# Batch norm over 64 tiles: moving columns between VectorE's first piece and ScalarE's piece

## The chip, the cores and the metric

The kernel runs on 1 core of one Trainium2 chip. The metric is the time of one launch in device microseconds (us), lower is better; a profiled execution also gives a span, from its first to its last instruction. The engines that do work here are VectorE (DVE in the profile), ScalarE (ACT), SyncE (SP, which only waits and issues transfers) and the core's 16 DMA engines, which move data between device memory and the on-chip buffers.

## The reference

```python
def setup_inputs():
    n = 32
    c = 256
    h = 128
    w = 128
    return {
        "x": np.random.randn(n, c, h, w).astype(np.float32),
...
def reference(
...
    eps = 1e-5
    mean = running_mean.reshape(1, -1, 1, 1)
    var = running_var.reshape(1, -1, 1, 1)
    gamma = gamma.reshape(1, -1, 1, 1)
    beta = beta.reshape(1, -1, 1, 1)
    return gamma * (x - mean) / np.sqrt(var + eps) + beta
```

With the statistics given, this is one multiply and one add for each element, with a scale and a shift for each channel. 537 MB are read and 537 MB written.

## The kernel before

The array is seen as 64 tiles (32 images by 2 blocks of 128 channels). A tile has 128 partitions, one channel each, and 16384 columns of float32, so a row is 64 KB and a tile 8.39 MB. Three buffers `bufs[0..2]` hold three tiles; tile i lives in buffer i mod 3 and is worked on in place. Ahead of the loop the kernel loads the parameters, turns them and computes `scale_t` and `shift_t` (lines 109 to 126); the first three tiles are loaded without a wait for a buffer (lines 90 to 99).

Four queues run after that, each in an order written out by hand, tied together by semaphores:

- VectorE (lines 155 to 158) works on a tile in two pieces. The first, columns 0 to `VFIRST`, waits until the tile has landed and raises `vfirst`. The second, columns `VFIRST` to `VMOST`, raises `vdone`. Tile 0 has one piece (`VHEAD` columns), and the last tile's second piece ends at `VLAST`.
- SyncE (lines 161 to 164) issues the load of tile i when the store of tile i - 3 is complete (line 163) and `vfirst` has been raised for tile i - 1 (line 164). So a load is issued only after the load ahead of it has landed and VectorE's first piece of it is done.
- ScalarE (lines 166 to 173) waits until the store of tile i - 1 is complete (line 168, all but the first and the last two tiles), does the columns from `VMOST` to the end, waits for `vdone` of tile i (line 170), and issues the store of tile i from its own queue (line 171).
- The loads run on the DMA queue that the profile calls q1, the stores on q10; both are spread over the same 16 DMA engines.

So at any time there is at most one load and one store under way. The length of VectorE's first piece lies between a load's landing and the next load's issue, and the length of ScalarE's piece lies between a store's completion and the next store's issue.

Of the kernel before, what the change touches and what calls it, by code (L numbers as in the profile page):

```python
# [8 lines left out]
NBUF = 3  # L9
PAD = 936  # L10
NHEAD = 3
VFIRST = 2560
VMOST = 14336
VHEAD = 8192
VLAST = 9216

# [2 lines left out]
def kernel(  # L19
# [54 lines left out]
    with tc.tile_critical():  # L74
# [26 lines left out]
        def landed(i):  # L101
            if i < NHEAD:
                return first[i], 16
            s = i % NBUF
            before = 1 if s < NHEAD else 0
            return loaded[s], 16 * (i // NBUF + 1 - before)
# [23 lines left out]
        def vector_part(i, first_col, end):  # L130
            t, cb = bufs[i % NBUF], i % NCB
            return nc.vector.tensor_scalar(  # L132
                out=t[:, first_col:end],
                in0=t[:, first_col:end],
                scalar1=scale_t[:, cb : cb + 1],
                scalar2=shift_t[:, cb : cb + 1],
                op0=mybir.AluOpType.mult,
                op1=mybir.AluOpType.add,
            )

        def scalar_part(i, first_col):
            t, cb = bufs[i % NBUF], i % NCB
            return nc.scalar.activation(  # L143
                out=t[:, first_col:],
                in_=t[:, first_col:],
                func=mybir.ActivationFunctionType.Identity,
                bias=shift_t[:, cb : cb + 1],
                scale=scale_t[:, cb : cb + 1],
            ).then_inc(adone, 1)

        def gone(i):
            return stored[i % NBUF], 16 * (i // NBUF + 1)
# [3 lines left out]
        for i in range(1, NT):  # L156
            vector_part(i, 0, VFIRST)._wait_ge(*landed(i)).then_inc(vfirst, 1)
            vector_part(i, VFIRST, VLAST if i == last else VMOST).then_inc(vdone, 1)

# [6 lines left out]
        for i in range(NT):  # L166
            if 0 < i < NT - 2:
                nc.scalar.wait_ge(*gone(i - 1))
            scalar_part(i, VHEAD if i == 0 else VLAST if i == last else VMOST)._wait_ge(*landed(i))
            nc.scalar.wait_ge(vdone, i + 1)  # L170
# [37 lines left out]
```

## Time and profile before

| what | value |
|---|---|
| time, median of 3 runs | 2486.29 us (2485.91 to 2487.04) |
| time of the profiled execution | 2487.21 us |
| its span | 2485.4 us |
| read and written | 536.94 MB and 536.87 MB, 432 GB/s over the span |
| median time from issue to landing | load 37.0 us, store 36.5 us |
| VectorE's pieces, columns and mean time | 2560: 1.61 us; 11776: 6.41 us |
| ScalarE's piece, columns and mean time | 2048: 2.09 us |

The profile's page lists busy time by engine, the DMA queues with the share of the 16 engines' time that their packets took, the chain of work that ended last, and groups of equal instructions by line with the idle time before them and what ended it (`<-DMA out_dram<-t` is a wait for a store, `<-DMA t<-in_x_dram` one for a load). In the rows in order of time, `ACTq` and `SPq` mark the issue of a transfer by ScalarE and SyncE, and x4 a row in which four are merged.

### The profile page before, as it was taken

The page shows a single profiled execution, that of the slowest core. Times are in us where ns is not written, and L with a number is a line of the kernel's source. Part 1 is how long each engine was busy: PE and PEld are TensorE (multiplying, and loading weights), DVE is VectorE, ACT ScalarE, POOL GpSimd, SP SyncE. Part 2 cuts the span into 40 slices and gives each one's busy share as a digit, 9 for nine tenths or more (in the row PEclk, how much of TensorE's full clock was granted, in tenths as well). Part 3 has the DMA queues.
Part 4 walks back from the last instruction along what each step waited for, and adds up shares of the span by engine and source line. Part 5 has one row for each costly group of instructions (what it writes and reads, how often), then busy time and mean ns, then how long its engine had stood idle before and what let it go on. Part 6 is the DMA issues. An engine that isn't in the chain of part 4 may idle for free.

```text
span 2485.4 us, 578 instructions
## 1 busy us (share of the span) xinstructions
DVE 505.3 (20%) x138; ACT 144.9 (6%) x66; POOL 0.2 (0%) x4
## 2 busy tenths in 40 slices
DVE  2122121221212212122121121211212212122120
ACT  1000000000000000000000000000000000000001
POOL 0000000000000000000000000000000000000000
DMA  9999999999999999999999999999999999999999
GB/s 421 424 439 438 422 439 433 428 438 436 426 438 437 425 438 437 428 436 436 437 427 437 436 427 438 431 429 439 423 438 437 433 429 436 437 428 437 435 428 405
DMA packets 18708, 1073.85 MB, mean 432 GB/s; under 512 B 2128, under 2 KB 2192, under 8 KB 2192
## 3 DMA queue, kind: packets, MB, share of 16 engines
q1 hardware_dynamic: 9488, 536.94, 50.0%
q10 hardware_dynamic: 9216, 536.88, 49.9%
q14 instruction: 4, 0.03, 0.0%
HBM read 536.94 MB, written 536.87 MB: 432 GB/s over the span
## 4 chain that ended last, share of the span: by engine, by line
DMA 93%; DVE 4%; another core or an unknown queue 1%; ACT 0%; issue 0%; SPq 0%; DVEq 0%
DMA t<-in_x_dram 93%; DVE t L132 4%; ACT t L143 0%; SPq L93 0%; DVE rows L91 0%; SPq L97 0%; DVE eps_t L109 0%; DVEq L203 0%; SPq L74 0%
## 5 line engine op out<-in xcount | busy, mean ns | idle before, releaser
L132 DVE TENSOR_SCALAR t<-t,scale_t,shift_t 128x11776 f32<-128x11776 f32 (+2 forms) x127 | 501.8, 3993 | 1938.8 <-DMA t<-in_x_dram 1938.7
L143 ACT ACTIVATE t<-t,shift_t,scale_t 128x2048 f32<-128x2048 f32 (+1 forms) x64 | 143.3, 2239 | 2299.2 <-DMA out_dram<-t 2243.3
L110 DVE STREAM_TRANSPOSE turned<-rows 32x1024 f32<-32x1024 f32 x1 | 1.2, 1232 | 12.0 <-DMA rows<-in_running_mean_dram 12.0
L116 ACT ACT_TABLE_LOAD x1 | 1.3, 1283 | 0.9 <-SPq L74 0.9
L91 DVE MEMSET rows<- 32x1024 f32 x1 | 0.9, 912 | 1.2 <-SPq L74 1.2
L116 ACT ACTIVATE std_t<-par,eps_t 128x2 f32<-128x2 f32 x1 | 0.3, 295 | 14.1 <-DVE par L114 14.1
L114 DVE COPY par<-turned 32x8 f32<-32x8 f32 x4 | 0.6, 162 | 0.1
L123 DVE RECIPROCAL rstd_t<-std_t 128x2 f32<-128x2 f32 x1 | 0.2, 165 | 0.4 <-ACT std_t L116 0.4
L125 DVE TENSOR_TENSOR ms_t<-par,scale_t 128x2 f32<-128x2 f32 x1 | 0.2, 161 | 0.0
L126 DVE TENSOR_TENSOR shift_t<-par,ms_t 128x2 f32<-128x2 f32 x1 | 0.2, 161 | 0.0
L124 DVE TENSOR_TENSOR scale_t<-par,rstd_t 128x2 f32<-128x2 f32 x1 | 0.2, 160 | 0.0
L192 POOL MEMSET const-bfloat16-1.0<- 128x1 bf16 x1 | 0.1, 101 | 0.0
L192 POOL MEMSET const-uint8-127<- 128x1 uint8 x1 | 0.1, 101 | 0.0
L192 POOL MEMSET const-float32-0.0<- 128x1 f32 x1 | 0.1, 98 | 0.2 <-issue 0.2
L192 POOL MEMSET const-float32-1.0<- 128x1 f32 x1 | 0.1, 98 | 0.0
L109 DVE MEMSET eps_t<- 128x1 f32 x1 | 0.1, 59 | 0.1
## 6 DMA issues: line engine op xcount, KB each, us to landing
t<-in_x_dram SPq DMA_DIRECT2D x2, 4096.0 KB, 15.9
out_dram<-t ACTq DMA_DIRECT2D x64, 36.5
t<-in_x_dram SPq DMA_DIRECT2D x63, 37.0
rows<-in_running_var_dram SPq DMA_DIRECT2D x1, 16.0 KB, 11.2
rows<-in_gamma_dram SPq DMA_DIRECT2D x1, 16.0 KB, 11.1
rows<-in_beta_dram SPq DMA_DIRECT2D x1, 16.0 KB, 10.8
rows<-in_running_mean_dram SPq DMA_DIRECT2D x1, 16.0 KB, 10.7
```

The lines of the kernel that those rows point to most:

```text
L91: zeroed = step(nc.vector.memset(rows[:], 0.0))
L109: step(nc.vector.memset(eps_t[:], eps))
L110: step(nc.vector.transpose(out=turned[:], in_=rows[:]), fetched, 16 * NPAR)
L114: placed = step(nc.vector.tensor_copy(out=flat[q * B : (q + 1) * B], in_=blocks[:, :, q, 0]))
L116: nc.scalar.activation(out=std_t[:], in_=var_t, func=mybir.ActivationFunctionType.Sqrt, bias=eps_t[:], scale=1.0,)._wait_ge(vec, placed).t ...
L123: step(nc.vector.reciprocal(out=rstd_t[:], in_=std_t[:]), act, 1)
L124: step(nc.vector.tensor_mul(out=scale_t[:], in0=gamma_t, in1=rstd_t[:]))
L125: step(nc.vector.tensor_mul(out=ms_t[:], in0=mean_t, in1=scale_t[:]))
L126: ready = step(nc.vector.tensor_sub(out=shift_t[:], in0=beta_t, in1=ms_t[:]))
L132: return nc.vector.tensor_scalar(out=t[:, first_col:end], in0=t[:, first_col:end], scalar1=scale_t[:, cb : cb + 1], scalar2=shift_t[:, cb ...
L143: return nc.scalar.activation(out=t[:, first_col:], in_=t[:, first_col:], func=mybir.ActivationFunctionType.Identity, bias=shift_t[:, cb : ...
L192: nc = _bacc.Bacc("TRN2", target_bir_lowering=False, num_devices=1)
```

## The change

Two constants. VectorE's first piece has 1696 columns in place of 2560 and its second 11136 in place of 11776; ScalarE's piece has 16384 - 12832 = 3552 columns in place of 2048. The first tile's pieces are as before; in the last tile the border between VectorE's two pieces moves with `VFIRST`.

```diff
--- before.py
+++ after.py
@@ -9,8 +9,8 @@
 NBUF = 3
 PAD = 936
 NHEAD = 3
-VFIRST = 2560
-VMOST = 14336
+VFIRST = 1696
+VMOST = 12832
 VHEAD = 8192
 VLAST = 9216
 
```

## The prediction

> **What bounds the kernel now.** I read the page's queue table first, then the chain of waits, then the groups of instructions, and last one stretch in order of time.
>
> ```profile
> span 2485.4 us, 578 instructions
> DVE 505.3 (20%) x138; ACT 144.9 (6%) x66; POOL 0.2 (0%) x4
> q1 hardware_dynamic: 9488, 536.94, 50.0%
> q10 hardware_dynamic: 9216, 536.88, 49.9%
> DMA t<-in_x_dram 93%; DVE t L132 4%; ACT t L143 0%; SPq L93 0%; DVE rows L91 0%; SPq L97 0%; DVE eps_t L109 0%; DVEq L203 0%; SPq L74 0%
> ```
>
> Loads (q1) take 50.0% and stores (q10) 49.9% of the time of the 16 DMA engines. Together that is 99.9%: they never stand still. The chain is loads, with VectorE's first piece (4%) between them. Taken alone it would say that a shorter first piece saves time; with the engines at 99.9% there is no time to save, only time to lose.
>
> ```profile
> L132 DVE TENSOR_SCALAR t<-t,scale_t,shift_t 128x11776 f32<-128x11776 f32 x62 | 397.2, 6407 | 0.0
> L143 ACT ACTIVATE t<-t,shift_t,scale_t 128x2048 f32<-128x2048 f32 x62 | 129.8, 2093 | 2250.8 <-DMA out_dram<-t 2243.3 <-DMA t<-in_x_dram 7.5
> L132 DVE TENSOR_SCALAR t<-t,scale_t,shift_t 128x2560 f32<-128x2560 f32 x63 | 101.6, 1612 | 1938.7 <-DMA t<-in_x_dram 1938.7
> L143 ACT ACTIVATE t<-t,shift_t,scale_t 128x8192 f32<-128x8192 f32 x1 | 7.2, 7212 | 6.8 <-DMA t<-in_x_dram 6.8
> L132 DVE TENSOR_SCALAR t<-t,scale_t,shift_t 128x8192 f32<-128x8192 f32 x1 | 4.5, 4546 | 0.1
> ```
>
> These are the groups with shapes kept apart (busy, mean ns of one, idle before). They price the change. In order of time:
>
> ```profile
> 1004.96 2.09 ACT L143 ACTIVATE t<-t,shift_t,scale_t 128x2048 f32<-128x2048 f32 x1 [36.56 <-DMA out_dram<-t]
> 1007.08 0.34 ACTq L171 DMA_DIRECT2D out_dram<-t  x1
> 1014.58 7.93 DVE L132 TENSOR_SCALAR t<-t,scale_t,shift_t 128x2560 f32<-128x2560 f32 x2 [30.69 <-DMA t<-in_x_dram]
> 1016.22 116.35 SPq L164 DMA_DIRECT2D t<-in_x_dram  x4
> 1043.71 2.09 ACT L143 ACTIVATE t<-t,shift_t,scale_t 128x2048 f32<-128x2048 f32 x1 [36.66 <-DMA out_dram<-t]
> ```
>
> Two loops run side by side. Store ends, ScalarE works 2.09 us, next store is issued (1007.08). Load ends, VectorE works 1.61 us, next load is issued (1016.22, the first of four merged into that row). Both have a period of 38.64 us (tiles 13 to 14, say). A tile is 128 rows of 64 KB each way, 8 load packets and 8 store packets for each of 16 engines, so a **slot** is 38.64/16 = 2.415 us; the trace's own packet records give 2.418 for nearly all of them. I chained those records, end to start, into 16 engines. In the steady state nearly every engine repeats this (L a load packet, S a store packet):
>
> ```
> LLLL SSSS LSLSLSLS LLLL SSSS LSLSLSLS ...
> ```
>
> So a store's turnaround is hidden by four load packets, and a load's by four store packets: 4 x 2.415 = 9.66 us each. Measured from the last packet's end on the last engine:
> - Store: 2.83 us to ScalarE's start, 2.09 of work, 0.04 to the issue: 4.96. Data then flows 2.85 to 3.3 after the issue. I take that from first store packets that began earlier than about 3.0 after their issue: they were stretched by up to 1.1 us, and ended as if begun at 2.8 to 3.3, a few of some 130 at 3.6 to 3.73; those that began later took the plain 2.418. Sum 7.8 to 8.3 of 9.66: 1.4 to 1.8 spare.
> - Load: 2.79 to VectorE's start, 1.61, 0.03: 4.43. It takes its turn in the alternation about 3.56 after the issue (3.4 to 3.75: the side on which engines give it a fifth store packet first, or not). Sum 7.99. To stay behind the fourth store packet it has to come after three, 3 x 2.415 = 7.245: 0.75 spare.
> The fixed distance of load issue after store issue agrees: 9.66 - 4.96 + 4.43 = 9.13, and 1016.22 - 1007.08 = 9.14.
>
> **The change part by part.**
> VectorE's first piece, 63 times: slope (4546 - 1612)/(8192 - 2560) = 0.521 ns a column, so 864 columns fewer are 1.612 - 0.450 = 1.162 us. The load is issued 3.98 after the load's end, takes its turn at 3.98 + 3.56 = 7.54, and the spare shrinks **from 0.75 to 0.29** (0.15 to 0.5 by the ends of that 3.4 to 3.75).
> VectorE's second piece, 62 times, 11136 columns: 6.407 - 640 x 0.000521 = 6.07 us. VectorE is through 7.2 us after a load lands, ScalarE begins that tile some 29 us after it (1014.58 to 1043.71): nothing. The last tile's second piece grows by 864 columns, 0.45 us, beside a first piece shorter by the same.
> ScalarE, 62 times: (7212 - 2093)/(8192 - 2048) = 0.833 ns a column, 1504 more: 2.093 + 1.253 = 3.346 us. Behind it on ScalarE's queue stand only the wait for VectorE (done by then) and the store's issue. The store is issued 6.21 after the store's end, and its data flows at 9.06 to 9.51 of 9.66: the spare shrinks **from 1.4-1.8 to 0.15-0.6**, and below nothing for those few at 3.6 to 3.73.
> The next load also waits for the store three tiles back: gone at about 1004.9, load issued at 1016.2, 11.3 us of cover; 1.25 of it goes. Instruction and DMA counts, bytes and SyncE's order stay.
>
> Added up while both stay covered: nothing, 2487.2 us (this execution's own time, span 2485.4 and 1.8 around it; 0.9 above the median of three).
>
> **Why I don't expect it to stay covered.** The two spares hang together. If a store's first packet starts late by w on an engine that ended its load among the last, its run of store packets is late too, while the load's turn is counted from the load's end. With w over 0.29 the load gets in after three store packets. Then that store's last packet comes at slot 13 in place of 12, only three load packets (7.245 us) are left to cover a turnaround of 9.06 to 9.51, and the engine stands for 1.8 to 2.3 us; the store is issued late for all 16, so all of them stand. And it keeps itself so: the load's turn, 7.54 after the load's end, falls 5.2 to 5.7 after the late store start, between two and three slots. Before, the same slip would leave 0.6 to 1.0 us of standing and put the load's turn at 7.0 to 7.4, at three slots, from where it can fall back.
> One such tile lasts 13 x 2.415 + 6.21 + 3.2 (the later of the 16 engines set it) = **40.8 us in place of 38.64, +2.2** (+1.8 by 2.85, +2.4 by 3.45).
> What sets it off is there in the trace: between store 4 and store 60 the period is 38.75 in the mean, some 6 us of slips, eight or so of 0.45 us or more (tiles 5, 15, 29, 38 and others). Each leaves the other engines waiting for the store's start, and of the packets that waited so, some 3% started later than 3.71, which is 0.26 too late. Over 15 engines that is about 35% a slip, so I put the fall after two or three slips, near tile 10: 52 tiles x 2.2 = 114 us, **2487.2 + 114 = 2601, so 2600**. Ends: from tile 2 on at +2.4, 148 us, 2635; from tile 40 on at +1.8, 40 us, 2527.
>
> **Rivals.**
> 1. *Covered anyway (not slower).* Spares of 0.29 and 0.15 to 0.6 are still spares; engines pushed late once line up and don't stand again. For: 99.9% busy, most first packets beginning after 3.05 show no stretch at all. Against: the slips. Time 2486 to 2492: narrower spares turn perhaps half of the 6 us of slips into as much again.
> The Trainium skill (DMA: Bandwidth & Descriptors, "Queues, rings and completion order") says that a DMA engine takes turns among the queues that have work, a whole packet at a time. The alternation above agrees; by that rule alone a turnaround costs nothing so long as the other queue has a packet waiting, which is this rival, and it decides against it only where four packets are no longer left.
> 2. *A slot further.* In the state of three, a start later than 3.7 after the issue loses another slot: 14 x 2.415 + 6.21 + 3.2 = 43.2, +4.6 a tile. Every engine waits in every tile there, so late starts have many chances; against it, an engine that stands may start sooner (the very first load, on idle engines, moved data 1.5 to 2.0 after its issue). 40 to 60 tiles: 2670 to 2763.
> 3. *The chain taken at its word (faster).* 62 x 0.45 = 28 us less, 2459. The engines' 99.9% excludes it; what can be won at all is the 6 us of slips, 2480.
>
> **How the numbers follow.** Forecast (state of three): 0.47, its own range 2527 to 2635. Rival 2: 0.19. Rival 1: 0.30, of which 0.23 lies within 0.2% (5 us; a measurement here tells no less from no change) and 0.07 just above. Rival 3: 0.04. Faster 0.04, same 0.23, slower 0.47 + 0.19 + 0.07 = 0.73. The range 2485 to 2740 leaves out rival 3, a little of rival 1 and the worst of rival 2.
>
> **What would show it.** ScalarE 128x3552 at 3.35 us and VectorE 128x1696 at 1.16 in the groups. Load issue after store issue: 9.66 - 6.21 + 3.98 = 7.43 us in the state of four, 5.02 in the state of three, 2.60 in that of two, with store periods of 38.6, 40.8 and 43.2. In the state of three GB/s fall to about 411 (434 x 38.64/40.8) from one tile on and stay there; the queues' shares need not fall with them, since a packet that waits is recorded as a long one, so the first packets of the stores should be stretched by 1.8 to 2.3 us. I am wrong if the distance is 7.43 to the end, or if it wanders with no fixed steps; and the mechanism is wrong if the time grows while first packets keep to 2.418 us and no engine stands.

## The result, and the profile after

The changed kernel takes 1.0591 times as long as before (95% interval 1.0573 to 1.0609). Of its six runs three took 2630.71 to 2634.13 us, which is what the ratio compares, one 2689.13 and two 2724.4 to 2724.8; the median of all six is 2661.63. Before: 2486.33 us, median of six. The forecast was 2600, slower. The profiled execution took 2633.49 us.

The page of the changed kernel, queues and chain, with the line of throughput in 40 slices:

```profile
span 2631.7 us, 578 instructions
DMA  9999999999999999999999999999999999999999
GB/s 415 430 414 398 413 399 398 415 405 407 415 398 414 406 406 411 401 414 404 408 412 401 414 398 414 406 406 413 399 415 398 414 398 406 406 413 399 414 399 413
q1 hardware_dynamic: 9488, 536.94, 49.9%
q10 hardware_dynamic: 9216, 536.88, 48.8%
DMA t<-in_x_dram 94%; DVE t L132 3%; ACT t L143 0%; SPq L93 0%; DVE rows L91 0%; SPq L97 0%; DVE eps_t L109 0%; DVEq L203 0%; SPq L74 0%
```

The same bytes take 146 us longer, and yet the DMA row is full of nines and the shares add up to 98.7%. A share counts a packet from its recorded start to its end, and a packet that waits for its data is just a long packet. The GB/s row shows the loss: about 407 from the third slice on, against some 433 before. The chain again names loads, 94%; ScalarE, whose piece does the harm as the experiments show, has 0% of it.

The groups with shapes kept apart cost what was worked out (3.346, 1.162 and 6.07 us were forecast):

```profile
L132 DVE TENSOR_SCALAR t<-t,scale_t,shift_t 128x11136 f32<-128x11136 f32 x62 | 376.6, 6074 | 0.0
L143 ACT ACTIVATE t<-t,shift_t,scale_t 128x3552 f32<-128x3552 f32 x62 | 207.5, 3347 | 2315.7 <-DMA out_dram<-t 2314.2 <-DMA t<-in_x_dram 1.5
L132 DVE TENSOR_SCALAR t<-t,scale_t,shift_t 128x1696 f32<-128x1696 f32 x63 | 73.2, 1162 | 2131.2 <-DMA t<-in_x_dram 2131.2
```

The first tiles of the changed kernel in order of time (start, length, engine, line; a DVE row has both pieces):

```profile
74.65 3.35 ACT L143 ACTIVATE t<-t,shift_t,scale_t 128x3552 f32<-128x3552 f32 x1 [44.04 <-DMA out_dram<-t]
78.03 0.34 ACTq L171 DMA_DIRECT2D out_dram<-t  x1
84.26 7.15 DVE L132 TENSOR_SCALAR t<-t,scale_t,shift_t 128x1696 f32<-128x1696 f32 x2 [24.15 <-DMA t<-in_x_dram]
85.45 77.43 SPq L164 DMA_DIRECT2D t<-in_x_dram  x3
113.42 3.35 ACT L143 ACTIVATE t<-t,shift_t,scale_t 128x3552 f32<-128x3552 f32 x1 [35.42 <-DMA out_dram<-t]
116.80 0.34 ACTq L171 DMA_DIRECT2D out_dram<-t  x1
120.61 7.15 DVE L132 TENSOR_SCALAR t<-t,scale_t,shift_t 128x1696 f32<-128x1696 f32 x2 [29.19 <-DMA t<-in_x_dram]
156.54 3.35 ACT L143 ACTIVATE t<-t,shift_t,scale_t 128x3552 f32<-128x3552 f32 x1 [39.77 <-DMA out_dram<-t]
```

Store 1 is issued at 78.03 and the next load at 85.45: a distance of 7.42, the forecast value (7.43) of the state in which four packets cover each turnaround. One tile later it is gone. VectorE starts only 3.81 us after the store's issue (116.80 to 120.61) in place of 6.23, so the load is issued a slot too early, and the store after that comes 43.1 us later in place of 38.6. In the middle of the run:

```profile
1025.22 0.34 ACTq L171 DMA_DIRECT2D out_dram<-t  x1
1026.56 7.15 DVE L132 TENSOR_SCALAR t<-t,scale_t,shift_t 128x1696 f32<-128x1696 f32 x2 [34.14 <-DMA t<-in_x_dram]
1027.74 82.46 SPq L164 DMA_DIRECT2D t<-in_x_dram  x3
1062.87 3.35 ACT L143 ACTIVATE t<-t,shift_t,scale_t 128x3552 f32<-128x3552 f32 x1 [37.68 <-DMA out_dram<-t]
1066.25 0.34 ACTq L171 DMA_DIRECT2D out_dram<-t  x1
```

The distance is 2.52 and the period 41.03 (1025.22 to 1066.25), and so it stays, 40.9 to 41.6 from tile 4 to the end. Some 59 tiles at 2.5 us make the 146.

The packet records show what tipped it. I chained them into 16 engines as in the prediction; behind a load's eight packets on an engine comes a small ninth, of 4 bytes, its completion: VectorE starts 0.31 to 0.52 us after the last of the 16, in both kernels. It stands in the load's queue and takes its turn with the store's packets like any other. So it follows the last load packet at once, or one slot (2.42 us) later if a store packet is served in between. In the kernel before, over 59 loads by 16 engines:

```
completion             engines   last load packet begins, us after the store's issue (5%, median, 95%)
at once  (before)        577        0.22   0.67   1.00
a slot later (before)    367        0.94   1.61   2.29
at once  (after)         936        nearly all before the store's issue
a slot later (after)       8
```

The border is sharp, just under 1 us (from store 4 of the changed kernel on, the first store packets are mostly recorded 0.84 to 1.04 us after the issue): a store whose issue lies further back has its packets waiting, and one of them goes ahead of the completion. Before, the last engines to finish a load were on the far side, so every load was reported a slot late. In the changed kernel the store comes 1.25 us later. For load 2 two of the 16 completions still were a slot late (83.8 against 81.1 to 81.6), and VectorE started at 84.26; for load 3 none was, all 16 came at 119.7 to 120.2, and it started at 120.61. A store's completion stands in the store's queue in the same way, but there a load packet goes ahead of it in both kernels, so ScalarE still starts about 2.83 us after the store's last packet.

```
before, tile 24     LLLL SSSS LSLSLSLS
after, tile 1       LLLL SSSS LSLSLSLS
after, tile 2       LLLL SSS LSLSLSLSLS
after, tile 24      LLL SSS LSLSLSLSLS    every engine; the store's packets wait
```

Theory A, then: *the load's completion comes a slot earlier, because the store comes later; the load is issued a slot early, and three load packets (7.245 us) are left for a store's turnaround of over 9.* The rivals are the prediction's own reason, slips between two narrow spares (B), and the chain taken at its word (C).

### The profile page after: what moved, and what is told of

Same layout as the page of the kernel before. It is cut to its first block, busy times and chain, and to the rows that moved or that the text cites. A ratio compares the mean times of both kernels' runs of the same rounds, so it can differ in the third digit from the quotient of the medians.

```text
span 2631.7 us, 578 instructions
## 1 busy us (share of the span) xinstructions
DVE 456.7 (17%) x138; ACT 222.6 (8%) x66; POOL 0.2 (0%) x4
## 4 chain that ended last, share of the span: by engine, by line
DMA 94%; DVE 3%; another core or an unknown queue 1%; ACT 0%; issue 0%; SPq 0%; DVEq 0%
DMA t<-in_x_dram 94%; DVE t L132 3%; ACT t L143 0%; SPq L93 0%; DVE rows L91 0%; SPq L97 0%; DVE eps_t L109 0%; DVEq L203 0%; SPq L74 0%
## 5 line engine op out<-in xcount | busy, mean ns | idle before, releaser
L132 DVE TENSOR_SCALAR t<-t,scale_t,shift_t 128x11136 f32<-128x11136 f32 (+2 forms) x127 | 453.2, 3611 | 2131.3 <-DMA t<-in_x_dram 2131.2
L143 ACT ACTIVATE t<-t,shift_t,scale_t 128x3552 f32<-128x3552 f32 (+1 forms) x64 | 221.1, 3454 | 2365.3 <-DMA out_dram<-t 2314.2
```

The source lines that it names most:

```text
L132: return nc.vector.tensor_scalar(out=t[:, first_col:end], in0=t[:, first_col:end], scalar1=scale_t[:, cb : cb + 1], scalar2=shift_t[:, cb ...
L143: return nc.scalar.activation(out=t[:, first_col:], in_=t[:, first_col:], func=mybir.ActivationFunctionType.Identity, bias=shift_t[:, cb : ...
```

## The experiments

**1. VectorE's part alone.**

```diff
-VFIRST = 2560
+VFIRST = 1696
```

> VectorE's part of the change alone (first piece 1696, ScalarE's piece 2048 as before). Theory A (turn of the completion): a load's completion write is a packet at the end of its queue and waits one slot behind a store packet, as long as the next store has arrived before the last load packet begins; here the store arrives as early as before, so nothing tips: distance of load issue after store issue 9.13 - 0.45 = 8.68 us, period 38.64, 2483 to 2490. Theory B (slips between two narrow spares, the prediction): load's spare 0.29 but store's spare 1.4 to 1.8, so a store start hardly ever comes late enough: 2486 to 2500. Theory C (the chain taken at its word): 62 x 0.45 = 28 us less, 2458.

2490.94 us (2482.70 to 2492.92), ratio 1.0017 (1.0007 to 1.0028). The distance is 8.7 and the period mostly 38.6 to 38.9. C falls. A and B both nearly hold; the 5 us lie a little over what A said, in B's range.

**2. ScalarE's part alone.**

```diff
-VMOST = 14336
+VMOST = 12832
```

> ScalarE's part alone (piece of 3552 columns, VectorE's first piece 2560 as before). Theory A: the store arrives 1.25 us later, after the last load packet has begun on most engines, so the load's completion goes ahead of it, a slot (2.42 us) earlier; the load takes its turn 0.36 + 1.61 + 0.03 + 3.56 = 5.6 us after its end, under three slots (7.245): state of three from the first tiles on, distance about 7.245 - 6.21 + 2.0 = 3.0 us, 2600 to 2680. Theory B: the load's spare is 0.75 as before, a store start is seldom 0.75 late: 2486 to 2500 and distance 7.88. Theory C: every store chain 1.25 us longer whatever the load does: 2486 + 62 x 1.25 = 2564.

2627.84 us (2622.42 to 2631.57), ratio 1.0567 (1.0550 to 1.0585). In order of time:

```profile
1022.72 0.34 ACTq L171 DMA_DIRECT2D out_dram<-t  x1
1024.07 7.15 DVE L132 TENSOR_SCALAR t<-t,scale_t,shift_t 128x2560 f32<-128x2560 f32 x2 [33.88 <-DMA t<-in_x_dram]
1025.71 41.41 SPq L164 DMA_DIRECT2D t<-in_x_dram  x2
1060.36 3.35 ACT L143 ACTIVATE t<-t,shift_t,scale_t 128x3552 f32<-128x3552 f32 x1 [37.67 <-DMA out_dram<-t]
1063.74 0.34 ACTq L171 DMA_DIRECT2D out_dram<-t  x1
```

Distance 2.99, where A said about 3.0 and B 7.88. (Tile 1 still has 7.89, tile 2 has 5.45: one slot less each time.) So ScalarE's longer piece alone makes the loss, with the load's spare as B counted it unchanged at 0.75. B falls, and C with its 2564. Of 944 completions 936 came at once, as in the changed kernel.

**3. Half as much more for ScalarE.**

```diff
-VMOST = 14336
+VMOST = 13312
```

> ScalarE's piece of 3072 columns (0.85 us longer than before), VectorE's first piece 2560. Before, the last load packet of the last engine begins 2.29 us after the store's issue; here 1.44 us after, and a store's packets can start 0.85 to 1.1 us after its issue. Theory A: still behind, so the completion keeps its turn: 2483 to 2495, distance 9.13 - 0.85 = 8.28. Theory B: store's spare 0.55 to 1.0, load's 0.75: 2486 to 2500, the same distance. Theory C: 62 x 0.85 = 53 us more, 2539.

A miss in part. Its ten runs fell apart: 2482.65 and 2484.59, five at 2504 to 2508, then 2636, 2646 and 2749; the ratio of the lower seven is 1.0057 (1.0030 to 1.0084). The profiled run (2484.59) kept a distance of 13.1, not 8.28, two slots (4.83) further: covered as well, with 928 of 944 completions a slot late. So 0.85 us more does not always tip it, but the margin is so thin that each run settles differently.

**4. The change, with the load released later.**

```diff
-VFIRST = 1696
+VFIRST = 6304
```

> ScalarE's piece of 3552 columns as in the change, but VectorE's first piece 6304 columns (3.56 us in place of 1.16), so that the load is released 2.4 us later. Theory A: the completion comes early, and the load's turn is 0.36 + 3.56 + 0.03 + 3.56 = 7.5 us after its end, past three slots again: state of four, distance 9.66 - 6.21 + 3.95 = 7.4 us, 2486 to 2510 although each release is later; where a completion keeps its turn behind a store packet the load is 0.3 us too late for four slots and that tile loses about as much. Theory B: the load's end to VectorE's start stays 2.79, its turn is at 9.94, past four slots: distance 9.83, some 0.3 us of standing a tile, 2505 to 2515. Theory C: a longer first piece is dearer still: 2633 + 63 x 2.4 = 2784.

Four runs: 2483.20, 2614.81, 2643.99, 2659.32. One run has the time back although the load is released *later*, which C excludes; it was not profiled. The other three lie far above A's 2510, so as a test of A this run is mostly a miss. In the one profiled (2659.32) the load falls further behind with every tile, from a distance of 9.8 in tile 1 and 14.7 in tile 2 to some 37 from tile 8 on, where both streams stand. The weak point had been named beforehand (a completion that does wait puts this load past four slots), but priced at some 0.3 us a tile.

**5. The change, with ScalarE's extra columns ahead of its wait.**

```diff
         for i in range(NT):
-            if 0 < i < NT - 2:
+            middle = 0 < i < NT - 2
+            if middle:
+                nc.scalar.activation(
+                    out=bufs[i % NBUF][:, VMOST : VMOST + 1504],
...
+                )._wait_ge(*landed(i))
                 nc.scalar.wait_ge(*gone(i - 1))
```

> The changed kernel's sizes, but ScalarE does 1504 of its 3552 columns before it waits for the store ahead and 2048 after, so that the store's turnaround is 2.09 us of work again. Theory A (the store's lateness lets the load's completion go ahead of it): all of the loss goes, as in VectorE's part alone: 2483 to 2495, distance 8.68 us, period 38.64. Theory B (slips between two narrow spares): the load's spare of 0.29 is left as in the change, the store's is 1.4 to 1.8: 2486 to 2500. Theory D (ScalarE's longer busy time or its access to the buffers costs, wherever it lies): 2630 as in the change.

2494.81 us (2485.46 to 2497.99), ratio 1.0034 (1.0024 to 1.0043).

```profile
1008.71 2.09 ACT L143 ACTIVATE t<-t,shift_t,scale_t 128x2048 f32<-128x2048 f32 x1 [27.82 <-DMA out_dram<-t]
1010.83 0.34 ACTq L180 DMA_DIRECT2D out_dram<-t  x1
1018.33 1.64 ACT L169 ACTIVATE t<-t,shift_t,scale_t 128x1504 f32<-128x1504 f32 x1 [7.52 <-DMA t<-in_x_dram]
1018.33 7.15 DVE L132 TENSOR_SCALAR t<-t,scale_t,shift_t 128x1696 f32<-128x1696 f32 x2 [31.92 <-DMA t<-in_x_dram]
1019.52 38.97 SPq L164 DMA_DIRECT2D t<-in_x_dram  x2
1047.36 2.10 ACT L143 ACTIVATE t<-t,shift_t,scale_t 128x2048 f32<-128x2048 f32 x1 [27.39 <-DMA out_dram<-t]
```

ScalarE does the same columns (3.74 us now, in two pieces), and the loss is gone but for 8.6 us: the distance is 8.69 (1010.83 to 1019.52), the period 38.65. D falls. What counts is ScalarE's work *between a store's end and the next issue*. The 8.6 us, as the 5 of the first run, come with VectorE's shorter first piece; B's spare of 0.29 against the slips could be their cause, but that was not separated.

**6 to 8. ScalarE's whole piece ahead of the wait,** with three lengths of VectorE's first piece (512, 2560 and then 1696 columns).

```diff
         for i in range(NT):
-            if 0 < i < NT - 2:
-                nc.scalar.wait_ge(*gone(i - 1))
             scalar_part(i, VHEAD if i == 0 else VLAST if i == last else VMOST)._wait_ge(*landed(i))
+            if 0 < i < NT - 2:
+                nc.scalar.wait_ge(*gone(i - 1))
```

> Both turnarounds at their shortest: ScalarE does all 3552 columns before it waits for the store ahead, and VectorE's first piece is 512 columns (0.54 us). Theory A, with its rule that load and store must be covered by equally many slots: store's turn about 2.9 + 3.56 = 6.5 us after its end, three slots; load's turn 2.79 + 0.54 + 0.03 + 3.56 = 6.9, under 7.245, three slots as well: covered, 2483 to 2495. Theory C (the shorter the two pieces on the chain, the better): the same or less, 2420 to 2486, down to 62 x 2.09 us less.

> ScalarE's columns all before the wait as in e6, but VectorE's first piece 2560 columns as in the kernel before. Theory A: store covered by three load packets (6.5 us of 7.245), load's turn 4.43 + 3.56 = 8.0, four store packets: unequal, so the stores run a slot ahead each tile until they have to wait for a load, and both streams stand at the same time: 2540 to 2700, although no turnaround is longer than in the kernel before. Theory C: the store's chain shorter by 2.09 us a tile and the load's as before: not slower than 2486.

> The changed kernel with only the order on ScalarE turned round: all 3552 columns before the wait for the store ahead, VectorE's first piece 1696 columns. Store's turn 6.5 us after its end: three load packets. Load's turn 3.98 + 3.56 = 7.54, past three slots (7.245) by 0.3, so four store packets where the completion waits its turn. Theory A with its rule of equally many slots: unequal, stores run ahead and then wait for loads, as with 2560 columns: 2560 to 2620. If the rule is wrong and only the length of the turnarounds counts, it lies between 512 and 2560 columns because its first piece does: about 2490 + (1.16 - 0.54)/(1.61 - 0.54) x 117 = 2558, and if only the store's turnaround counts 2484 to 2500.

512 columns: 2490.50 us (2483.74 to 2519.51), ratio 1.0031 (1.0003 to 1.0058). 1696: 2589.91 us, 1.0421 (1.0406 to 1.0437). 2560: 2607.43 us, 1.0492 (1.0472 to 1.0512). C falls hard: with 2560 columns VectorE has what it had in the kernel before, ScalarE has *nothing* left to do between stores, and the kernel is 5% slower. The waits of that run (waiter, what for, total, times, longest) and its order of time:

```profile
ACT t L143 <- DMA t<-in_x_dram: 2346.8, 64, 40.2
DVE t L132 <- DMA t<-in_x_dram: 2112.6, 63, 36.4
...
1029.47 3.35 ACT L143 ACTIVATE t<-t,shift_t,scale_t 128x3552 f32<-128x3552 f32 x1 [37.29 <-DMA t<-in_x_dram]
1029.47 7.15 DVE L132 TENSOR_SCALAR t<-t,scale_t,shift_t 128x2560 f32<-128x2560 f32 x2 [33.49 <-DMA t<-in_x_dram]
1031.11 39.88 SPq L164 DMA_DIRECT2D t<-in_x_dram  x2
1036.73 0.34 ACTq L171 DMA_DIRECT2D out_dram<-t  x1
```

In this order ScalarE's piece waits for a load only. The stores, covered by three slots, ran ahead of the loads, which need four: the distance grows from 14.4 us in tile 1 to 33.4 in tile 5, by some 4.8 us, two slots, a tile, where one slot had been expected. Then the stores have caught up; from tile 6 to tile 60 a store is issued 0.11 us after VectorE's second piece, every time. A load lands (1029.4), and VectorE's 7.15 us pass before the store of the same tile is issued, with both queues empty for part of that. 1696 columns, with a load's turn at 7.54, do the same (13.2 us in tile 1, 32.7 in tile 5, then some 34). In time, too, they are nearer to 2560 than to 512 columns (6.9); the straight line through the piece's length would have put them at 2558. That fits a border at three slots, 7.245.

The 512 columns are not firm. Their slowest run is 36 us over their fastest, and that slowest one, the only one profiled, does not show A's equal counts: its distance steps up as well, more slowly, 17.6 in tile 1, 27.2 in tile 5 and 32 to 33 from tile 18 on, where it too has its stores close behind VectorE. So that unequal counts lose time is seen in two traces; that equal counts of three keep it rests on the times of the faster runs alone.

**9 and 10. The change with still longer ScalarE pieces,** 4576 and 5600 columns.

```diff
-VMOST = 12832
+VMOST = 11808        # 10784 in the second
```

> The changed kernel with ScalarE's piece another 1024 columns longer (4576; 0.853 us). In the state of three the store's loop is 13 slots, ScalarE's work and the fixed parts, so every tile takes 0.85 us more: Theory A and B: 2633 + 61 x 0.85 = 2685 (2675 to 2700) with the same three load packets, distance 2.6 - 0.85 = 1.7 us. Theory E (the state's loss comes from how loads and stores share the DMA engines, not from the store's loop): about 2633 as in the change.

> The changed kernel with ScalarE's piece of 5600 columns (5.05 us, another 0.85 us over 4576 columns). Theory F: the 2720 us of the 4576-column run, and the runs of the changed kernel near 2724, are a second state in which the load waits for its buffer and is issued the moment a store is complete; its loop is 16 slots (38.64) + 0.45 to completion + some 3 us until the load's data flows, about 42.4 us a tile whatever ScalarE's length, as long as the store is there when three load packets are through: 2715 to 2730, flat. Theory B (13 slots plus ScalarE's work set the tile): 0.85 us more a tile, 2720 + 52 = 2772.

2720.30 us (ratio 1.0946, 1.0929 to 1.0962) and 2732.36 us (1.0999, 1.0974 to 1.1024). The first missed: A and B expected 2685 and E 2633. Another state had come, shown here for 5600 columns:

```profile
1015.60 6.09 DVE L132 TENSOR_SCALAR t<-t,scale_t,shift_t 128x1696 f32<-128x1696 f32 x2 [36.87 <-DMA t<-in_x_dram]
1020.80 43.22 SPq L164 DMA_DIRECT2D t<-in_x_dram  x2
1020.82 5.05 ACT L143 ACTIVATE t<-t,shift_t,scale_t 128x5600 f32<-128x5600 f32 x1 [37.71 <-DMA out_dram<-t]
1025.90 0.34 ACTq L171 DMA_DIRECT2D out_dram<-t  x1
```

VectorE's first piece is long over (1015.60), yet the load is issued at 1020.80, the moment ScalarE too learns that a store is complete: it waits for its buffer. (SyncE's waits for a buffer's store, line 163, add up to 2606 us here, those for VectorE to 13; with 4576 columns it is 2596 and 12.) The loop is then 16 slots, the completion and the load's own start, and ScalarE's length hardly enters: 0.85 us more cost 12 us, where 61 tiles of it are 52. Theory F holds nearly. The two runs of the changed kernel at 2724 us fit this state (4576 columns: 2720), but no trace of them was taken, so that is argued, not shown.

**11. The other way: a shorter ScalarE piece.**

```diff
-VMOST = 14336
+VMOST = 15360
```

> The other way: ScalarE's piece 1024 columns (1.24 us, 0.85 less than before), VectorE's first piece 2560 as before. Theory A: the store arrives 0.85 us earlier, so nearly all of the loads' last packets begin more than 0.95 us after its issue and their completions wait a slot on nearly every engine (39% of them did before); the load's turn stays at 7.99, the store's moves to 2.83 + 1.24 + 0.04 + 3.56 = 7.7, still past three slots: state of four, distance 9.98, 2482 to 2488, at best the slips are fewer and it gains up to 4 us. Theory C (every microsecond between stores counts): 62 x 0.85 = 53 us less, 2433.

2483.16 us (2481.96 to 2492.16), ratio 1.0000 (0.9991 to 1.0009). C falls once more. 936 of 944 completions came a slot late, as A said; the distance was 14.8 and not 9.98, again two slots further. Its median is 2.4 us under that of the kernel before in the same session (2485.55), which the interval does not tell from nothing. So no version was found that beats the kernel before.

## Why the prediction was right, and where it was wrong

*What bounds the kernel:* right, though the share of 99.9% does not show it by itself: the changed kernel's shares still add up to 98.7%, and 6% is lost. The packets' lengths show it: 97.6% of the 64 KB packets took the plain 2.418 us before, 76.8% after. And none of eleven variants won anything that can be told from none, though six shortened a piece on the chain or between stores and lengthened neither.

*Slots of 2.415 us, four by four, distances 9.13 and 7.43:* right; tile 1 of the changed kernel is at 7.42.

*"2.79 to VectorE's start":* this is the step that failed. I took the time from a load's last packet to VectorE's start as fixed. It is 0.36 us and, if a store's packet goes first, one slot more. The changed store takes that slot away, so the load's turn moved not from 7.99 to 7.54 but to 0.36 + 1.16 + 0.03 + 3.56 = 5.1, well under three slots.

*"What sets it off", slips, near tile 10:* wrong for that reason. No slip was needed: in the profiled run it fell at tile 2. (The slips were also fewer than the "eight or so": only four store periods before, those at tiles 5, 15, 29 and 38, are 0.45 us or more over 38.64.) Whether slips would have tipped it later, had the completion kept its turn, no run shows. And the fall needs only ScalarE's half of the change (second run); VectorE's half costs 5 us.

*The state of three, +2.2 us a tile:* the pattern is right, the size a little low. The steady period is 41.2, which is 13 slots (31.40), a store's turnaround (2.86 + 3.35 + 0.03 = 6.24) and 3.55 until data flows on the last of the 16 engines, where I had put 3.2. 2.5 us over 59 tiles are 148, where I had 2.2 over 52, 114. That 2600 came within 1.3% of 2633 is in part luck: the state and most of its price were right, but not what led into it, and the fall had been expected from slips that had no part in it.

*"5.02 in the state of three":* wrong, by the same slot; it is 5.0 for tile 2 alone and about 2.5 to 2.65 from tile 3 on, since the completion now comes at once. Read by the distance alone this would have passed for my state of two (2.60); only the packets show three. The waiting was recorded partly as a gap ahead of the store's first packet, and partly on the third store packet and the load packet behind it, not on the first packet as I had said.

*Rival 1, covered anyway:* it fell; its rule, turns packet by packet, is right, and applied to the completion it would have pointed to what happened. *Rival 2, a slot further:* its price range, 2670 to 2763, holds three of the six runs, but none of these was profiled, and in the profiled run its mechanism is not seen. *Rival 3:* excluded: run 1 and runs 6 to 8 and 11 shortened one chain or the other and gained nothing.

## What to carry to other kernels

When two streams share full DMA engines, ask of each whether its turnaround, in whole packets of the other, is covered, and by how many. Where the counts differed here (2560 and 1696 columns in runs 6 to 8), the faster stream ran ahead until it had to wait for the other, both stood at once, and 4 to 5% were lost. Work between a completion and the next issue was free here up to an edge and dear beyond it; what isn't needed there goes ahead of the wait, but see to the other stream's count as well. Don't judge such a kernel by busy shares: look at GB/s and at the distance between the two issues.

## What the hardware showed that I had not expected

A load's completion takes its turn among the packets of the other queue: 0.36 us from the last packet's end to VectorE's start where no store packet is waiting, 2.79 where one is, in one and the same kernel (loads 62 and 63 of the changed one). The Trainium skill (DMA: Bandwidth & Descriptors, "Anatomy of one DMA — SWDGE (gpsimd) path") puts most of the fixed 2 us of a DMA issued by GpSimd down to the confirmation of the last write. The loads here are issued by SyncE, and 2.42 of their 2.79 us are another queue's packet.

Kernels that differ only in these constants settled in one of several steady patterns, and near an edge the same kernel settled differently from run to run: 3072 columns took 2482.65 to 2748.59 us.
